# Token inputs laid out by feature on the host for a decoder layer on one core, in place of transposes at the kernel's start

## The chip, the cores and the metric

The kernel runs on one core of one Trainium2 chip. The metric is the device time of one execution in microseconds (us); lower is better. TensorE is PE in the rows of the profile (PEld is its weight load), VectorE is DVE, ScalarE is ACT, GpSimd is POOL and SyncE is SP. SP computes nothing here: it issues loads and stores, one after the other, and an issue that must wait holds up the issues behind it.

## The reference

One decoder layer on 256 tokens of 2048 features. Sixteen learned meta tokens are put in front, so 272 tokens go through the layer, and the sixteen are dropped at the end. All is float32.

```
s = concat(meta_tokens, x)                                   # 272 x 2048
h = rms_norm(s, norm_ffn1)
s = s + 0.5 * (silu(h @ w_gate_part) * (h @ w_up_part)) @ ffn1_w_down      # F = 5632
h = rms_norm(s, norm_mix)
q, k, v, b_gate, c_gate, u = split(h @ w_in)
y_att  = diff_attention(q, k, v, lam, subln)    # lam from four vectors of 64
y_conv = b_gate * conv3(c_gate * u, conv_w)
merged = sum over both branches of sigmoid(h @ w_gate) * (y @ w_branch)
s = s + merged @ w_out
h = rms_norm(s, norm_ffn2)
s = s + 0.5 * swiglu_ffn(h, ffn2_w_gu, ffn2_w_down)
out = rms_norm(s, norm_final)[16:]
```

The first product, `h @ ffn1_w_gu`, is where the change works; `ffn1_w_gu` is 2048 x 11264.

## The kernel before

**Layout.** The activations stand with features on the 128 partitions and tokens along the row: `sF[g]` holds four blocks of 128 features (chunks) by 272 tokens, and `s(c, t0)` is chunk c of 16. Products run with weights as the stationary operand, 128x128, and 272 tokens as the moving one.

**Two parts per operand.** Float32 values are split into a high and a low part, each in the format fp32r, and a product is made of three passes: high x high, low x high, high x low (lines 367 to 369). For weights, ACT makes the high part `wh` by a cast (lines 345 and 351) and DVE the low part `wl` by a subtraction (line 356). For activations `gain_split` multiplies by the norm's gain and splits: ACT makes the high part (line 231), DVE the low one (line 232). The factor of the norm that belongs to a token, `rstd`, is applied later, on the product.

**The first product.** `linear` walks 16 chunks of features and, for each, 4 blocks of 128 outputs: 16 x 4 x 3 = 192 passes, accumulated in four PSUM banks `pg`. In this first call a function `before1` prepares the activations while the product runs: chunk 0 alone, chunk 1 alone, then chunks in twos, each pair with one weight load `st` of 512 KB, one cast of 128x1024 and one subtraction of 128x1024. In the text below a pair is named by its chunks ("weights 2-3"). The squares for the norm are summed on the way: ACT squares a chunk (line 250), DVE adds it (line 252). After the last pass a product with ones (`ssq`, line 257) sums over partitions, and the next product, `pu`, starts at once.

**How the tokens come in.** x lies in memory by token. `load_x` brings 128 tokens by some chunks of features into `xin`; `prep` turns each 128x128 block by a transpose on PE (line 733) into the bank `pt`, and DVE copies it to `sF` (line 739). There are 16 chunks x 2 halves of the tokens = 32 such transposes and 16 copies. The meta tokens are turned two blocks at a time (line 724, bank `pm`) and copied in eight small pieces (line 727); the gain of the first norm is loaded as 16 rows and turned too (line 141). The other vectors (two norms, the convolution, `subln`) come by four small loads later, into `vrows`, and are turned in one transpose in `make_vec` (line 154) about 686 us into the run.

**What orders the start.** A scheduler orders instructions per engine from the program's order and the releases of buffers. SP's queue carries x and the weights alternately; ACT's queue carries the meta tokens and the gain. Seven products of ones (`keep_warm`, line 86) run on PE from the start, and two more behind the first transposes. There are four buffers `st`, three each of `wh` and `wl`, and eight PSUM banks.

**Names of the change.** `load_x`, `X_LOADS` (which chunks are loaded when), `prep`, `prep_meta`, `before1`, `load_vectors`, `make_vec`, `make_lam`.

Of the kernel before, what the change touches and what calls it, by code (L numbers as in the profile page):

```python
# [9 lines left out]
F32 = mybir.dt.float32  # L10
# [5 lines left out]
P = 128  # L16
D = 2048
SEQ = 256
NMETA = 16
# [3 lines left out]
GC = 4  # L23
# [14 lines left out]
N_AUX = 3  # L38
EVICT_AT = 1
WARM = 7  # L40
WARM_PREP = 2
HOLD = 6
LATER_AT = (4, 6)

# [16 lines left out]
def decoder_layer(ctx: ExitStack, tc: tile.TileContext, t, out):  # L61
# [9 lines left out]
    def bank(name):  # L71
        return psum.tile([P, 512], F32, tag="acc", name=name)
# [11 lines left out]
    def keep_warm(n):  # L84
        for _ in range(n):
            nc.tensor.matmul(warm[:, :P], ones, ones, start=True, stop=True)
# [1 line left out]
    keep_warm(WARM)  # L88


    grow = const.tile([DC, P], F32, name="grow")
    x = t["x"][0]
# [20 lines left out]
    vrows = const.tile([NV, P], F32, name="vrows")  # L113
    G_MIX, G_FFN2, G_CONV, G_SUB = 0, DC, 2 * DC, NV - 1

    lamv = tmp.tile([P, 4, HD], F32, tag="sc", name="lamv")
# [27 lines left out]
    vec = const.tile([P, NV], F32, name="vec")  # L144

    def col(i):
        return vec[:, i : i + 1]

    lam = const.tile([P, 40], F32, name="lam")[:, 0:1]
    subg = const.tile([P, 1], F32, name="subg")  # L150

    def make_vec():
        vp = bank("vp")
        nc.tensor.transpose(vp[:, :NV], vrows, ident[:NV, :NV])
# [14 lines left out]
    sF = [apool.tile([P, GC, T], F32, tag="act", name=f"s{g}") for g in range(DC // GC)]  # L169

    def s(c, t0, t1=T):
        return sF[c // GC][:, c % GC, t0:t1]

    class Act:

# [51 lines left out]
    def gain_split(h, c, gain):  # L227

        w = h.width
        hi, lo = h.part(c, 0, 0, w), h.part(c, 1, 0, w)  # L230
        a = nc.scalar.mul(hi, s(c, T - w), gain)  # L231
        b = nc.vector.scalar_tensor_tensor(  # L232
            out=lo, in0=s(c, T - w), scalar=gain, in1=hi.bitcast(F32), op0=ALU.mult, op1=ALU.subtract
        )
        return a.ins, b.ins
# [478 lines left out]
    h1 = Act("h1", DC, T, range(NH), PIECE)  # L714
    norm1 = Norm(0, "1")

    pm, split_of, turned = [], [], []

    def prep_meta(g):

        if not pm:
            pm.append(bank("pm"))
            for j in range(2):
                nc.tensor.transpose(pm[0][:, j * P : (j + 1) * P], xm[:, j * P : (j + 1) * P], ident)
        for j in range(2):
            cols = pm[0][:, j * P : (j + 1) * P].rearrange("p (t g) -> p g t", t=NMETA)
            nc.vector.tensor_copy(sF[g][:, j:GC:2, :NMETA], cols[:, 2 * g : 2 * g + 2, :])

    def prep(c):
        pt = bank("pt")  # L730
        q, cs = c // NH, slice(c % NH * P, (c % NH + 1) * P)
        for i in range(2):
            turned.append(nc.tensor.transpose(pt[:, i * P : (i + 1) * P], xin[q][i][:, cs], ident).ins)
        if c % GC == 0:
            prep_meta(c // GC)
        with ExitStack() as order:
            if c in (2, 3):
                order.enter_context(tc.issue_after(split_of[1]))
            v = nc.vector.tensor_copy(s(c, NMETA), pt[:, :SEQ])
        a, b = gain_split(h1, c, gain1[:, c : c + 1])  # L740
        split_of.append(b)
        return a, v.ins

    X_LOADS = {2: (2, 2), 4: (4, 4), 8: (8, 4), 10: (12, 4)}

    def before1(blk):


        c = blk[0]
        if c in X_LOADS:  # L750
            load_x(*X_LOADS[c])
        r = []
        for k in blk:
            a, v = prep(k)
            r = [a, v]
            if k == 0:
                r.append(split_of[0])
                with tc.issue_after(turned[-1]):
                    keep_warm(WARM_PREP)
        for k in blk:  # L760
            if k >= 2:
                norm1.add(k - 2)
        if c == DC - 2:
            for k in blk:
                norm1.add(k)
            pending.append(norm1.end)
        return r
# [538 lines left out]


_INS = [
    "x", "meta_tokens", "norm_ffn1", "ffn1_w_gu", "ffn1_w_down", "norm_mix", "w_in", "conv_w", "lambda_q1",
    "lambda_k1", "lambda_q2", "lambda_k2", "subln", "w_branch", "w_gate", "w_out", "norm_ffn2", "ffn2_w_gu",  # L1310
    "ffn2_w_down", "norm_final",
]


# [16 lines left out]
```

## Time and profile before

| what | value |
|---|---|
| runs of the kernel | 2149.14 us median of 3 (2148.92 to 2149.18) |
| profiled execution, span from first to last instruction | 2147.3 us |
| granted TensorE clock, mean | 0.999 |
| PE busy | 2137.4 us, 13202 instructions |
| DVE busy | 1611.9 us |
| ACT busy | 1105.5 us |
| bytes by DMA | 439.70 MB, mean 205 GB/s |

For the profiled execution itself only the span is on the page; the median of the runs is 1.84 us above it, which is what lies outside the first and last instruction. A busy share of an engine is a mean over the whole run; the change works in the first 37 us, and once at 686 us, so views restricted to a window are what to read. Starts are in us from the span's start. Consecutive instructions on an engine overlap at their ends, so the cost of one in a row of many is the distance from its start to the next start, which is a little less than its duration.

### The profile page before, as it was taken

To read this page: it belongs to the slowest core of one execution; us is meant where nothing else is said; L and a number is where in the kernel's file an instruction comes from. 1 tells how busy PE (TensorE), PEld (TensorE's weight loads), DVE (VectorE), ACT (ScalarE), POOL (GpSimd) and SP (SyncE) were. 2 spreads that over 40 slices of the span, in tenths; PEclk is the share of its full clock that TensorE was granted. 3 is DMA by queue.
4 is the path that set the end of the run, shared out by engine and by line. 5 is a ranking of instruction groups with operands and counts; after the bars stand their busy time and mean duration, and the time that the engine had idled before them with its cause. 6 is when DMAs were issued, how large, how long until landed. Compare 5 with 4: busy or idle time off the path is not lost.

```text
span 2147.3 us, 33079 instructions
## 1 busy us (share of the span) xinstructions
PE 2137.4 (100%) x13202; PEld 1929.1 (90%) x13202; DVE 1611.9 (75%) x2139; ACT 1105.5 (51%) x1391; POOL 79.4 (4%) x89
## 2 busy tenths in 40 slices
PE   9999999999999999999999999999999999999998
PEld 9999999999999998899988888888888888888887
DVE  8555554445555668867887889889999899988998
ACT  6344443344333455545545555557665566555665
POOL 0000000000000000000000000001100111012100
PEclk9999999999999999999999999999999999999999
DMA  7555555555555555544455555668886999779963
GB/s 258 177 177 178 177 181 177 178 180 179 180 180 176 178 178 187 190 157 142 154 189 186 198 201 187 216 206 256 267 259 198 286 285 277 234 219 311 287 207 138
DMA packets 200544, 439.70 MB, mean 205 GB/s; under 512 B 10493, under 2 KB 11206, under 8 KB 200390
## 3 DMA queue, kind: packets, MB, share of 16 engines
q1 hardware_dynamic: 184022, 398.13, 54.9%
q0 software_dynamic: 15904, 38.80, 8.2%
q8 instruction: 103, 1.69, 0.3%
q10 hardware_dynamic: 464, 0.66, 0.1%
q14 instruction: 51, 0.42, 0.1%
HBM read 431.26 MB, written 2.10 MB: 202 GB/s over the span
## 4 chain that ended last, share of the span: by engine, by line
PE 98%; DVE 1%; DMA 0%; ACT 0%; issue 0%; SPq 0%; ACTq 0%
PE pg L569 6%; PE pg L571 6%; PE pg L570 6%; PE pd L369 4%; PE pd L367 4%; PE pu L367 4%; PE pu L368 4%; PE pu L369 4%; PE pd L368 4%; PE pg L367 4%; PE pg L368 4%; PE pg L369 4%; PE pd L571 4%; PE pd L570 4%; PE pd L569 4%; PE g L571 2%
## 5 line engine op out<-in xcount | busy, mean ns | idle before, releaser
L356 DVE TENSOR_TENSOR wl<-st,wh 128x1024 fp32r<-128x1024 f32 (+1 forms) x329 | 401.1, 1221 | 378.4 <-ACT wh L351 378.3
L351 ACT CAST wh<-st 128x1024 fp32r<-128x1024 f32 (+1 forms) x328 | 343.0, 1047 | 487.4 <-PE pu L368 151.0
L476 DVE TENSOR_TENSOR wl<-st,wh 128x1024 fp32r<-128x1024 f32 (+1 forms) x424 | 470.9, 1118 | 55.4 <-ACT wh L475 52.3
L475 ACT CAST wh<-st 128x1024 fp32r<-128x1024 f32 (+1 forms) x424 | 400.3, 970 | 208.8 <-PE pdx L570 60.5
L475 ACT CAST wh<-t 128x1024 fp32r<-128x1024 f32 x160 | 166.6, 1052 | 242.5 <-DVE t L609 162.3
L476 DVE TENSOR_TENSOR wl<-t,wh 128x1024 fp32r<-128x1024 f32 x160 | 193.8, 1222 | 56.3 <-ACT wh L475 51.7
L369 PE MATMUL pd<-mh,wl 128*128 128x272 f32 x704 | 203.1, 288 | 0.0
L367 PE MATMUL pd<-mh,wh 128*128 128x272 f32 x704 | 202.3, 287 | 0.0
L367 PE MATMUL pu<-h,wh 128*128 128x272 f32 x704 | 201.9, 287 | 0.0
L367 PE MATMUL pg<-h,wh 128*128 128x272 f32 x704 | 201.6, 287 | 0.2 <-ACT h L231 0.2
L369 PE MATMUL pu<-h,wl 128*128 128x272 f32 x704 | 201.7, 287 | 0.0
L368 PE MATMUL pu<-h,wh 128*128 128x272 f32 x704 | 201.7, 286 | 0.0
L368 PE MATMUL pg<-h,wh 128*128 128x272 f32 x704 | 201.2, 287 | 0.1
L368 PE MATMUL pd<-ml,wh 128*128 128x272 f32 x704 | 200.7, 285 | 0.0
L369 PE MATMUL pg<-h,wl 128*128 128x272 f32 x704 | 199.6, 287 | 0.1
L570 PE MATMUL pg<-wh,h 128*128 128x512 f32 x399 | 156.0, 391 | 0.0
L569 PE MATMUL pg<-wh,h 128*128 128x512 f32 x399 | 155.8, 390 | 0.0
L571 PE MATMUL pg<-wl,h 128*128 128x512 f32 x399 | 155.7, 391 | 0.0
L368 PEld LDWEIGHTS pd<-ml,wh 128*128 128x128 f32 x704 | 133.5, 190 | 0.0
L367 PEld LDWEIGHTS pg<-h,wh 128*128 128x128 f32 x704 | 132.6, 188 | 0.7 <-ACT h L231 0.4
L368 PEld LDWEIGHTS pg<-h,wh 128*128 128x128 f32 x704 | 132.6, 188 | 0.3 <-DVE h L232 0.3
L368 PEld LDWEIGHTS pu<-h,wh 128*128 128x128 f32 x704 | 132.6, 188 | 0.0
(391 smaller groups left out, 4839.6 us busy)
## 6 DMA issues: line engine op xcount, KB each, us to landing
st<-in_ffn_w_gu_dram SPq DMA_DIRECT2D x183, 512.0 KB, 6.0
st<-in_ffn_w_down_dram SPq DMA_DIRECT2D x88, 1024.0 KB, 5.1
st<-in_ffn_w_gu_dram SPq DMA_DIRECT2D x84, 1024.0 KB, 4.9
st<-in_w_in_dram SPq DMA_DIRECT2D x48, 1024.0 KB, 5.1
st<-in_w_gate_dram SPq DMA_DIRECT2D x64, 512.0 KB, 4.1
t<-in_ffn_w_gu_dram POOLq DMA_DIRECT2D x64, 512.0 KB, 7.0
st<-in_w_branch_dram SPq DMA_DIRECT2D x32, 512.0 KB, 4.5
st<-in_w_out_dram SPq DMA_DIRECT2D x16, 1024.0 KB, 5.2
```

The lines of the kernel that those rows point to most:

```text
L351: nc.scalar.copy(out=wh[:, :m, :], in_=sw)
L356: nc.vector.tensor_sub(wl[:, :m, :], sw, wh[:, :m, :].bitcast(F32))
L367: nc.tensor.matmul(a, wh[:, i, f], act.part(c, 0, t0, t1), start=first, stop=False)
L368: nc.tensor.matmul(a, wh[:, i, f], act.part(c, 1, t0, t1), start=False, stop=False)
L369: nc.tensor.matmul(a, wl[:, i, f], act.part(c, 0, t0, t1), start=False, stop=last)
L475: part_last[:] = [nc.scalar.copy(out=wh, in_=src).ins]
L476: part_last.append(nc.vector.tensor_sub(wl, src, wh.bitcast(F32)).ins)
L569: nc.tensor.matmul(ps[k], hi, wh, start=first, stop=False)
L570: nc.tensor.matmul(ps[k], lo, wh, start=False, stop=False)
L571: nc.tensor.matmul(ps[k], hi, wl, start=False, stop=left[k] == 0)
```

## The change

The host now hands over x and the meta tokens as one array of 128 x 16 x 272 (partition, chunk, token), the gain of the first norm as 128 x 16, and the other vectors as one array of 128 x 57. `load_x` writes straight into `sF`; the transposes, the banks and the copies are gone, and so are the two extra products of ones. The first chunk of x comes on ACT's queue, after the gain; all others on SP's queue. (Line numbers of the new kernel are smaller: line 99 is `load_x`, 205 and 206 are the two halves of `gain_split`, 226 the addition of squares, 311 the weight load, 325 the cast, 330 the subtraction, 341 to 343 the three passes.)

```diff
-WARM_PREP = 2
...
-    xm = apool.tile([P, 2 * P], F32, tag="act", name="xm")
-    xin = [[apool.tile([P, W2], F32, tag="act", name=f"xin{q}{i}") for i in range(2)] for q in range(2)]
...
-    def load_x(c, n):
-
-        q, cs = c // NH, slice(c % NH * P, (c % NH + n) * P)
-        for i in range(2):
-            x_load[:] = [
-                nc.sync.dma_start(out=xin[q][i][:, cs], in_=x[i * P : (i + 1) * P, c * P : (c + n) * P]).ins
-            ]
-
-    load_x(0, 2)
-    meta_load = nc.scalar.dma_start(out=xm, in_=t["meta_tokens"].rearrange("t (g f) -> (t g) f", f=2 * P))
-    with tc.issue_after(meta_load.ins):
-        nc.scalar.dma_start(out=grow, in_=t["norm_ffn1"][0].rearrange("(c p) -> c p", p=P))
+    def load_x(c, n, eng=None):
+        dst = sF[c // GC][:, c % GC : c % GC + n, :]
+        ins = (eng or nc.sync).dma_start(out=dst, in_=x[:, c : c + n, :]).ins
+        if eng is None:
+            x_load[:] = [ins]
+
+    gain1 = const.tile([P, DC], F32, name="gain1")
+    nc.scalar.dma_start(out=gain1, in_=t["gain1"])
+    load_x(0, 1, nc.scalar)
...
     def load_vectors():
-        for g0, src in ((G_MIX, t["norm_mix"][0]), (G_FFN2, t["norm_ffn2"][0])):
-            nc.sync.dma_start(out=vrows[g0 : g0 + DC, :], in_=src.rearrange("(c p) -> c p", p=P))
-        nc.sync.dma_start(
-            out=vrows[G_CONV:G_SUB, :], in_=t["conv_w"][0].rearrange("k (c p) -> (k c) p", p=P)
-        )
-        nc.sync.dma_start(out=vrows[G_SUB:NV, :], in_=t["subln"])
+        nc.sync.dma_start(out=vec, in_=t["vectors"])
...
-    gp = bank("gp")
-    nc.tensor.transpose(gp[:, :DC], grow, ident[:DC, :DC])
-    gain1 = const.tile([P, DC], F32, name="gain1")
-    nc.vector.tensor_copy(gain1, gp[:, :DC])
...
-    def make_vec():
-        vp = bank("vp")
-        nc.tensor.transpose(vp[:, :NV], vrows, ident[:NV, :NV])
-        nc.vector.tensor_copy(vec, vp[:, :NV])
...
     def prep(c):
-        pt = bank("pt")
-        q, cs = c // NH, slice(c % NH * P, (c % NH + 1) * P)
-        for i in range(2):
-            turned.append(nc.tensor.transpose(pt[:, i * P : (i + 1) * P], xin[q][i][:, cs], ident).ins)
-        if c % GC == 0:
-            prep_meta(c // GC)
-        with ExitStack() as order:
-            if c in (2, 3):
-                order.enter_context(tc.issue_after(split_of[1]))
-            v = nc.vector.tensor_copy(s(c, NMETA), pt[:, :SEQ])
-        a, b = gain_split(h1, c, gain1[:, c : c + 1])
-        split_of.append(b)
-        return a, v.ins
-
-    X_LOADS = {2: (2, 2), 4: (4, 4), 8: (8, 4), 10: (12, 4)}
+        return gain_split(h1, c, gain1[:, c : c + 1])
+
+    X_LOADS = {0: (1, 1), 1: (2, 2), 2: (4, 2), 4: (6, 2), 6: (8, 4), 8: (12, 4)}
...
         for k in blk:
-            a, v = prep(k)
-            r = [a, v]
-            if k == 0:
-                r.append(split_of[0])
-                with tc.issue_after(turned[-1]):
-                    keep_warm(WARM_PREP)
+            r = list(prep(k))
...
-            side.extend((make_vec, make_lam))
+            side.append(make_lam)
...
+    tokens = np.concatenate([a["meta_tokens"], a["x"][0]], axis=0)
+    d["x"] = tokens.T.reshape(DC, P, T).transpose(1, 0, 2)
```

Three places of the program show how rows move. The first is SP's queue at the start of the program. `xin` holds tokens by token, `s` is the tile `sF`, `st` a weight load; 128x256 is a row of 1 KB per partition. Before:

```order
L104 DMA xin_90<-in_x_dram 128x256
L104 DMA xin_91<-in_x_dram 128x256
L337 DMA st<-in_ffn_w_gu_dram 128x512 x2
L104 DMA xin_90<-in_x_dram 128x256
L104 DMA xin_91<-in_x_dram 128x256
L337 DMA st<-in_ffn_w_gu_dram 128x2x512
```

And now:

```order
L311 DMA st<-in_ffn_w_gu_dram 128x512
L99 DMA s_88<-in_x_dram 128x272
L99 DMA s_88<-in_x_dram 128x544
L311 DMA st<-in_ffn_w_gu_dram 128x512
L99 DMA s_89<-in_x_dram 128x544
L311 DMA st<-in_ffn_w_gu_dram 128x2x512
```

The first weights come ahead of x, and three pieces of x (chunks 1, 2-3 and 4-5) stand ahead of weights 2-3, where four pieces (chunks 0-1 and 2-3, two each) stood before.

The second place is PE's start. `warm` is the bank of the products of ones. Before:

```order
L86 MATMUL warm<-ones 128x128 x7
L141 MATMUL gp<-ident,grow 128x16
L733 MATMUL pt<-ident,xin_90 128x128
L733 MATMUL pt<-ident,xin_91 128x128
L724 MATMUL pm<-ident,xm 128x128 x2
L86 MATMUL warm<-ones 128x128 x2
L733 MATMUL pt<-ident,xin_90 128x128
L733 MATMUL pt<-ident,xin_91 128x128
L367 MATMUL pg_145<-h_116,wh 128x272
```

And now:

```order
L85 MATMUL warm<-ones 128x128 x7
L341 MATMUL pg_133<-h_104,wh 128x272
L341 MATMUL pg_134<-h_104,wh 128x272
L341 MATMUL pg_135<-h_104,wh 128x272
L341 MATMUL pg_136<-h_104,wh 128x272
L342 MATMUL pg_133<-h_104,wh 128x272
```

Between the seven products of ones and the first real pass PE has nothing left to do.

The third place is DVE's queue behind its two memsets, where `norm` is the sum of squares. Before:

```order
L143 COPY gain_107<-gp 128x16
L739 COPY s_112<-pt 128x256
L727 COPY s_112<-pm 128x2x16 x2
L727 COPY s_113<-pm 128x2x16 x2
L232 SCALAR_TENSOR_TENSOR h_116<-s_112,gain_107,h_116 128x272
L356 TENSOR_TENSOR wl<-st,wh 128x512
L739 COPY s_112<-pt 128x256
```

And now:

```order
L206 SCALAR_TENSOR_TENSOR h_104<-s_88,gain_92,h_104 128x272
L330 TENSOR_TENSOR wl<-st,wh 128x512
L206 SCALAR_TENSOR_TENSOR h_104<-s_88,gain_92,h_104 128x272
L330 TENSOR_TENSOR wl<-st,wh 128x512
L206 SCALAR_TENSOR_TENSOR h_105<-s_88,gain_92,h_105 128x272 x2
L226 TENSOR_TENSOR norm<-norm 128x272
L330 TENSOR_TENSOR wl<-st,wh 128x1024
```

What is left on DVE is the low parts and the additions, in the same order among themselves up to small shifts.

More of the change, by code (lines that the diff above doesn't have):

```diff
@@ L88, in decoder_layer, with s @@
     keep_warm(WARM)
-    grow = const.tile([DC, P], F32, name="grow")
-    x = t["x"][0]
-    xm = apool.tile([P, 2 * P], F32, tag="act", name="xm")
-    xin = [[apool.tile([P, W2], F32, tag="act", name=f"xin{q}{i}") for i in range(2)] for q in range(2)]
+    x = t["x"]
     x_load = []
-    def load_x(c, n):
-        q, cs = c // NH, slice(c % NH * P, (c % NH + n) * P)
-        for i in range(2):
-            x_load[:] = [
-                nc.sync.dma_start(out=xin[q][i][:, cs], in_=x[i * P : (i + 1) * P, c * P : (c + n) * P]).ins
-            ]
-    load_x(0, 2)
-    meta_load = nc.scalar.dma_start(out=xm, in_=t["meta_tokens"].rearrange("t (g f) -> (t g) f", f=2 * P))
-    with tc.issue_after(meta_load.ins):
-        nc.scalar.dma_start(out=grow, in_=t["norm_ffn1"][0].rearrange("(c p) -> c p", p=P))
+    sF = [apool.tile([P, GC, T], F32, tag="act", name=f"s{g}") for g in range(DC // GC)]
+    def s(c, t0, t1=T):
+        return sF[c // GC][:, c % GC, t0:t1]
+    def load_x(c, n, eng=None):
[6 more added lines that the diff above has]
+    load_x(0, 1, nc.scalar)
     NV = 2 * DC + 3 * NH + 1
-    vrows = const.tile([NV, P], F32, name="vrows")
     G_MIX, G_FFN2, G_CONV, G_SUB = 0, DC, 2 * DC, NV - 1
+    vec = const.tile([P, NV], F32, name="vec")
     lamv = tmp.tile([P, 4, HD], F32, tag="sc", name="lamv")
     def load_vectors():
-        for g0, src in ((G_MIX, t["norm_mix"][0]), (G_FFN2, t["norm_ffn2"][0])):
-            nc.sync.dma_start(out=vrows[g0 : g0 + DC, :], in_=src.rearrange("(c p) -> c p", p=P))
-        nc.sync.dma_start(
-            out=vrows[G_CONV:G_SUB, :], in_=t["conv_w"][0].rearrange("k (c p) -> (k c) p", p=P)
-        )
-        nc.sync.dma_start(out=vrows[G_SUB:NV, :], in_=t["subln"])
+        nc.sync.dma_start(out=vec, in_=t["vectors"])
         for i, n in enumerate(("lambda_q1", "lambda_k1", "lambda_q2", "lambda_k2")):
@@ L1308, with _by_partition, _laid_out @@
 _INS = [
-    "x", "meta_tokens", "norm_ffn1", "ffn1_w_gu", "ffn1_w_down", "norm_mix", "w_in", "conv_w", "lambda_q1",
-    "lambda_k1", "lambda_q2", "lambda_k2", "subln", "w_branch", "w_gate", "w_out", "norm_ffn2", "ffn2_w_gu",
-    "ffn2_w_down", "norm_final",
-]
+    "ffn1_w_gu", "ffn1_w_down", "w_in", "lambda_q1", "lambda_k1", "lambda_q2", "lambda_k2", "w_branch", "w_gate",
+    "w_out", "ffn2_w_gu", "ffn2_w_down", "norm_final",
+]
+def _by_partition(np, a):
+    rows = a.reshape(-1, a.shape[-1] // P, P)
+    return np.ascontiguousarray(rows.reshape(-1, P).T)
+def _laid_out(np, inputs):
+    a = {k: np.asarray(v) for k, v in inputs.items()}
+    d = {name: a[name] for name in _INS}
+    tokens = np.concatenate([a["meta_tokens"], a["x"][0]], axis=0)
+    d["x"] = tokens.T.reshape(DC, P, T).transpose(1, 0, 2)
+    d["gain1"] = _by_partition(np, a["norm_ffn1"])
+    d["vectors"] = np.concatenate(
+        [_by_partition(np, v) for v in (a["norm_mix"], a["norm_ffn2"], a["conv_w"][0], a["subln"])], axis=1
+    )
+    return d
 def kernel(**inputs):
@@ L1321 @@
     arrays, args = {}, {}
-    for name in _INS:
-        a = _np.ascontiguousarray(inputs[name])
+    for name, a in _laid_out(_np, inputs).items():
+        a = _np.ascontiguousarray(a)
         arrays[f"in_{name}_dram"] = a
```

13 lines of the change are left out of this document (removed).

## The prediction

> **What bounds the kernel.** I read the page first, for which engine the run hangs on.
>
> ```profile
> span 2147.3 us, 33079 instructions
> ...
> PE 98%; DVE 1%; DMA 0%; ACT 0%; issue 0%; SPq 0%; ACTq 0%
> ```
>
> The chain that ended last runs over PE for 98% of the span. So whatever shortens PE's queue, or lets it start earlier, comes off the end, unless something else becomes late. The 2% that are not PE lie mostly at the start; the same chain, restricted to the first 37 us, shows what:
>
> ```profile
> 1.19 3.06 DMA xin<-in_x_dram
> ...
> 4.66 6.65 DMA xin<-in_x_dram
> ...
> 11.35 0.34 PE pt L733
> ...
> 12.47 0.72 DVE wl L356
> ...
> 30.42 0.34 DVE s L739
> ...
> 36.13 0.46 PE ssq_ps L257 x2
> 36.59 0.12 PE pu L367
> ```
>
> First a load of x sets the pace (its second piece lands at 11.3), then for 19 us DVE, with copies from `pt` (L739) among the low parts, and from there PE. The next product starts at 36.59. Two windows over PE's passes, of `pu` and of `pg` from chunk 2 on, tell what the stage costs beyond its products:
>
> ```profile
> 36.59:60.30 23.71, 23.68 (x192) 23.46 (x191) 0.80 (x3) 1.00 0.61 205
> 12.09:36.13 24.04, 22.64 (x168) 21.18 (x168) 0.00 (x0) 0.00 (x0) 1.00 0.81 281
> ```
>
> With nothing in the way 192 passes take 23.71 us, 0.1235 each. Chunks 2 to 15 are 168 passes, 20.75 us at that rate, but stand from 12.09 to 36.13, 24.04 us: 3.3 us go to transposes and waits. After 36.59 PE is never short of work for long, so I take the start of `pu` as the finish line: the run ends as much earlier as `pu` starts earlier.
>
> **The change, part by part.** *Transposes on PE.* The timeline of PE:
>
> ```profile
> 1.06 3.35 PE L86 MATMUL warm<-ones 128*128 128x128 f32 x14 [1.06 <-DVE ones L80]
> 4.56 0.69 PE L733 MATMUL pt<-ident,xin 128*128 128x128 f32 x2
> 5.46 0.66 PE L86 MATMUL warm<-ones 128*128 128x128 f32 x4
> 5.96 0.38 PE L733 MATMUL pt<-ident,xin 128*128 128x128 f32 x2
> 6.51 0.39 PE L367 MATMUL pg<-h,wh 128*128 128x272 f32 x1 [0.16 <-ACT h L231]
> 8.87 0.60 PE L733 MATMUL pt<-ident,xin 128*128 128x128 f32 x4
> 10.88 0.27 PE L733 MATMUL pt<-ident,xin 128*128 128x128 f32 x1
> 11.35 0.98 PE L733 MATMUL pt<-ident,xin 128*128 128x128 f32 x7 [0.20 <-DMA xin<-in_x_dram]
> 12.09 0.37 PE L367 MATMUL pg<-h,wh 128*128 128x272 f32 x1
> ```
>
> A lone transpose shows 0.27, seven in a row 0.98, so one more costs (0.98 - 0.27) / 6 = 0.118 us. Up to 12.09 there are 2 + 2 + 4 + 1 + 7 = 16 of 32; the other 16 lie in the window from 12.09, 1.9 us. Of its 3.3 us that leaves 1.4 us of waits.
>
> *Copies on DVE.* The DVE timeline gives the price of each kind by the distance of starts:
>
> ```profile
> 12.39 1.22 DVE L356 TENSOR_TENSOR wl<-st,wh 128x1024 fp32r<-128x1024 f32 x1
> ...
> 23.55 0.90 DVE L232 SCALAR_TENSOR_TENSOR h<-s,gain,h 128x272 fp32r<-128x272 f32 x2
> 24.38 0.43 DVE L252 TENSOR_TENSOR norm<-norm 128x272 f32<-128x272 f32 x1
> 24.73 1.21 DVE L356 TENSOR_TENSOR wl<-st,wh 128x1024 fp32r<-128x1024 f32 x1
> 25.87 0.43 DVE L252 TENSOR_TENSOR norm<-norm 128x272 f32<-128x272 f32 x1
> 26.22 0.74 DVE L739 COPY s<-pt 128x256 f32<-128x256 f32 x2
> 26.89 0.42 DVE L252 TENSOR_TENSOR norm<-norm 128x272 f32<-128x272 f32 x1
> ...
> 34.10 1.22 DVE L356 TENSOR_TENSOR wl<-st,wh 128x1024 fp32r<-128x1024 f32 x1
> ```
>
> A low part of h is 0.415, an addition 0.35, a subtraction 1.14, a copy 0.335. From 12.39 to the end of the subtraction at 34.10 (35.3) DVE has 8 x 1.14 + 12 x 0.415 + 14 x 0.35 + 10 x 0.335 = 22.4 us of work in 22.9: it is full, and nearly as long as PE's stage. Without the copies 19.0 are left, under PE's 20.75, so behind chunk 2 the bound passes to PE. Not all 1.4 us of waits go: a pair's eight passes with `wh` last 1.0 us, while its subtraction, which the ninth pass needs, takes 1.14 behind the cast, so where cast and pass come due together 0.2 to 0.35 is lost; I count two such places and keep 0.6. Two numbers follow: the finish line lies 20.75 + 0.6 + 0.46 (`ssq`) = 21.8 us behind the first pass of chunk 2, against 36.59 - 12.09 = 24.5 before. Gain: 2.7 us, with 1.9 to 3.3 as bounds (only the transposes, or no wait at all).
>
> *Start of chunk 2.* Before, 12.09. Now it hangs on weights 2-3, which must land and be cast. The cast, from the ACT timeline, and the loads, from the view of DMA issues (x's first piece, weights 2-3) and SP's timeline:
>
> ```profile
> 10.93 1.03 ACT L351 CAST wh<-st 128x1024 fp32r<-128x1024 f32 x1
> ...
> xin<-in_x_dram SPq DMA_DIRECT2D x1, 128.0 KB, 3.0
> st<-in_ffn_w_gu_dram SPq DMA_DIRECT2D x1, 512.0 KB, 5.7
> ...
> 3.73 0.38 SPq L337 DMA_DIRECT2D st<-in_ffn_w_gu_dram  x1
> ```
>
> Weights 2-3 were issued at 3.73 and landed at 9.43. What SP's queue moved, counted from 0 to 5.5, 6.5, 7, 8 and 9 us (packets, MB):
>
> ```profile
> q1 hardware_dynamic: 564, 0.75, 49.3%
> q1 hardware_dynamic: 828, 1.04, 55.5%
> q1 hardware_dynamic: 928, 1.19, 59.4%
> q1 hardware_dynamic: 1109, 1.53, 64.1%
> q1 hardware_dynamic: 1245, 1.79, 67.8%
> ```
>
> Before, weights 2-3 ended 1536 KB of that queue (x 512, weights 1024), 1.57 MB, moved by 8.1; they landed 1.3 us later. Now they end 1704 KB (weights 256, x 136 and 272, weights 256, x 272, weights 512), 1.75 MB, moved by 8.8 at the same pace, so they land at 10.1. Counted in rows of a partition instead, it is 896 now against 1024 before: reached at 6.85 and 7.5, so that they would land about 8.7. The two views differ because the rows of x are now longer. From 5.5 to 6.5 us, with rows of 1 KB among them, 264 packets carried 0.29 MB, from 7 to 8 us 181 carried 0.34: the packets differ by half, the bytes by a sixth, so bytes are nearer to what limits, and I take 9.8. With 1.05 for the cast chunk 2 starts at 10.85: gain 1.25, bounds 2.3 (rows) and 0.6 (0.3 later by bytes, and the slower clock below).
>
> *The first pass.* At 6.51 before. Now the first weights are first in SP's queue and chunk 0 second in ACT's; by the 3.0 us above, and the 1.19 + 3.06 in the chain for a second piece, both land by about 4.3, cast and high part follow, and the first pass comes at 5.4. That 1.1 us is not added: chunks 0 and 1 end by 10 either way, and chunk 2 waits for its weights. SP's issue times don't bind, since weights 2-3 are its sixth issue.
>
> *Late vectors.* One transpose less at 686 us, and the wait of DVE for the last small load, in the rows of `vp` and of `lamv`:
>
> ```profile
> L154 PE MATMUL vp<-ident,vrows x1: 269/269/269, 685.6 to 685.6; 57*128 57x57 f32 x1
>   DMA lamv<-in_lambda_k_dram: 0.4, 1
> ```
>
> The transpose is worth 0.1 us by the price above. Four small loads become one, and the scaled `subln` now comes on DVE at 277 us, next to the product that waited 0.4 us there; three loads fewer ahead of it can only shorten that. PE covers it; uncovered it costs 0.4. The gain's load of 64 bytes per partition stands ahead of chunk 0 on ACT's queue, where 8 KB stood behind the meta tokens; 8 KB either way, taken at nothing, and at most the 1.1 us of the first pass.
>
> *Sum.* 2.7 + 1.25 + 0.1 = 4.05 us off the profiled span of 2147.3, and so off the median, 1.84 above it: 2149.14 - 4.05 = 2145.1. 0.2% of the time, 4.3 us, is about what a measurement of this kernel can tell from no change, so the likeliest case lies just inside it.
>
> **Rivals.** *Loads go by rows.* Weights 2-3 land at 8.7, chunk 2 starts at 9.75, and the gain is 2.3 + 2.7 + 0.1 = 5.1: 2144.0. For it: the new rows of x are 1 to 4 KB where half of the early rows were 1 KB. Against: the counts of packets and bytes above.
>
> *Late or slow first chunks.* The passes of ones run 3.35 / 14 = 0.24 us each at 1.06, and four of them take 0.66 at 5.46, (0.66 - 0.27) / 3 = 0.13: PE got twice as fast at about 5.3, though the granted clock reads 1.00 throughout. Now PE has nothing between 4.4 and 5.4, and gaps again around chunks 0 and 1. If it is at half rate there, 24 passes of 0.247 from 5.4 end at 11.5 with a small wait, so chunk 2 starts at 11.5: gain 0.6 + 2.7 + 0.1 = 3.4, 2145.7. If it stays so for 14 more passes, 1.7 us go and the gain is 1.7: 2147.4. The Trainium skill, "TensorE: Matmul & The Clock Gate", section "What's actually happening", has the array at half rate until about 3.4 us of sustained work fill a window that runs freely, and again after an idle window. This trace agrees as to the factor and roughly as to the time, 4.2 us from the first pass; by that rule the idle microsecond may or may not spoil the window, and the second variant would be one more window.
>
> *Slower.* The same mechanism, but without recovery: PE keeps half rate until the product is dense. Each pass then costs 0.12 more; from 11.5 on 28 passes eat the gain (to 18.4 us), and 62 make it slower by 0.2% (to 27 us). At 30 us it would be 75 passes, 9.3 us: 2155.0. Against it: the passes from 11.5 on are dense, and before the change 4.2 us of them were enough.
>
> *The transposes were hidden anyway.* If x's loads bound the start as before and chunk 2 starts at 12.09, only 2.8 are gained: 2146.3. The chain above speaks for loads at the start, but weights 2-3 landed at 9.43, and it was x that came at 11.3.
>
> **How the numbers follow.** As forecast (gain 3.5 to 4.6): 0.45. By rows (4.6 to 5.7): 0.25. Slow first chunks or late loads (1.5 to 3.5): 0.26. Slower: 0.04. The range takes the first two whole and the third down to a gain of 2.3: 2143.4 to 2146.8. Faster by over 0.2% is the second case and some 0.4 of the first: 0.42. Slower by over 0.2%: 0.03. The rest, 0.55, within it.
>
> **What would show it.** `pu` starts at 32.6 instead of 36.59; chunk 2's first pass at 10.85, released by ACT's cast, and that by the load of weights 2-3; DVE idle at times between 12 and 32 instead of full; passes of chunks 0 and 1 about 0.12 apart (0.25 for the slow clock). Wrong it would be if weights 2-3 land before 9 or after 11, if DVE remains the chain's engine behind chunk 2, or if anything behind `pu` shifts by more than some tenths.

## The result and the profile after

The changed kernel takes 2144.64 us (median of 13 runs, 2144.09 to 2144.95) where the kernel before took 2149.09 in the same session (13 runs, 2148.78 to 2150.06): a ratio of 0.9979, 95% interval 0.9972 to 0.9986, or 4.45 us less. The forecast was 2145.1, with 4.05 us less. The profiled execution of the changed kernel is the quickest of its 13 (2144.09 us), so the two profiled spans lie 5.0 us apart instead of 4.45; sums over the two traces are made against 5.0.

The page of the changed kernel: its span, the busy times, and the engines on the chain that ended last.

```profile
span 2142.3 us, 32969 instructions
...
PE 2132.4 (100%) x13162; PEld 1925.7 (90%) x13162; DVE 1604.8 (75%) x2113; ACT 1105.5 (52%) x1391; POOL 79.3 (4%) x89
...
PE 99%; DMA 0%; DVE 0%; ACT 0%; issue 0%; ACTq 0%
```

The chain restricted to the first 36 us has nothing of DVE left in it. It is one load of x, the high part of chunk 0 on ACT, and from 5.02 on PE without a gap (start, length, what):

```profile
1.18 3.17 DMA s<-in_x_dram
4.44 0.53 ACT h L205
5.02 1.27 PE pg L341 x4
...
9.69 0.18 PE pg L342
9.88 0.13 PE pg L343
...
31.17 0.46 PE ssq_ps L231 x2
```

The timeline of PE gives the first pass, its releaser, the first pass of chunk 2, and the two landmarks at the end of the stage, displayed by start:

```profile
5.02 1.27 PE L341 MATMUL pg<-h,wh 128*128 128x272 f32 x4 [0.60 <-ACT h L205]
...
10.22 0.28 PE L341 MATMUL pg<-h,wh 128*128 128x272 f32 x1
...
31.00 0.62 PE L231 MATMUL ssq_ps<-norm,ones 128*128 128x272 f32 x2
31.26 0.49 PE L341 MATMUL pu<-h,wh 128*128 128x272 f32 x1
```

Before, the same timeline has:

```profile
35.97 0.62 PE L257 MATMUL ssq_ps<-norm,ones 128*128 128x272 f32 x2
36.23 0.49 PE L367 MATMUL pu<-h,wh 128*128 128x272 f32 x1
```

So `pu` starts 4.97 us earlier, and the spans differ by 5.0: what lies behind `pu` did not change by more than the 0.1 that the spans are given to. Two windows over the passes of `pg` (length, then busy time and count on PE, PEld, DVE, ACT, the granted clock, DMA share, GB/s) show where the stage is short and where it is not:

```profile
5.02:9.70 4.68, 4.68 (x20) 4.68 (x21) 0.00 (x0) 0.00 (x0) 1.00 1.05 392
...
10.40:31.13 20.73, 20.73 (x168) 20.54 (x167) 0.00 (x0) 0.00 (x0) 1.00 0.92 329
```

The 168 passes of chunks 2 to 15 take 20.73 us, the 0.1235 apiece of a PE that waits for nothing. (Their first starts at 10.22 in the timeline, while the pass ahead of it still ends; the window begins where that one has ended. Below, chunk 2 is put at 10.22, since the 12.09 of the kernel before is a start in the timeline too.) The first 20 passes take 0.234 each, though the granted clock reads 1.00: PE was at half rate until 9.7. And DVE, with no copies, is no longer full. The same stretch before (first row) and after (second; columns PE, PEld, DVE, ACT, POOL):

```profile
12.00:31.00 19.00, 18.74 (x153) 18.37 (x151) 19.00 (x40) 13.87 (x29) 0.00 (x0) 1.00 0.80 290
```

```profile
12.00:31.00 19.00, 19.00 (x155) 18.99 (x155) 16.71 (x30) 14.88 (x29) 0.00 (x0) 1.00 0.91 322
```

Weights 2-3, whose landing the forecast put at 9.8, were issued on SP's queue at 3.07 and took 5.2 us, so they landed at 8.27, and their cast followed at once. The rows are from SP's timeline, the view of DMA issues and ACT's timeline:

```profile
3.07 0.43 SPq L311 DMA_DIRECT2D st<-in_ffn_w_gu_dram  x1
```

```profile
st<-in_ffn_w_gu_dram SPq DMA_DIRECT2D x1, 512.0 KB, 5.2
```

```profile
8.26 1.04 ACT L325 CAST wh<-st 128x1024 fp32r<-128x1024 f32 x1
```

The cast ended at 9.3, and PE, busy with chunks 0 and 1 until then, took chunk 2 at 10.22.

### The profile page after: what moved, and what is told of

The parts are those of the page before. It is cut to its first block, busy times and chain, and to the rows that moved or that the text cites. A ratio compares the mean times of both kernels' runs of the same rounds, so it can differ in the third digit from the quotient of the medians.

```text
span 2142.3 us, 32969 instructions
## 1 busy us (share of the span) xinstructions
PE 2132.4 (100%) x13162; PEld 1925.7 (90%) x13162; DVE 1604.8 (75%) x2113; ACT 1105.5 (52%) x1391; POOL 79.3 (4%) x89
## 4 chain that ended last, share of the span: by engine, by line
PE 99%; DMA 0%; DVE 0%; ACT 0%; issue 0%; ACTq 0%
PE pg L543 6%; PE pg L545 6%; PE pg L544 6%; PE pd L343 4%; PE pg L341 4%; PE pg L343 4%; PE pg L342 4%; PE pd L341 4%; PE pu L341 4%; PE pu L343 4%; PE pu L342 4%; PE pd L342 4%; PE pd L545 4%; PE pd L544 4%; PE pd L543 4%; PE g L545 2%
```

## The experiments

The theory after this reading: the gain is a start about 1.5 us earlier and the transposes gone from PE; PE's half rate at the start took the place of waits that vanished. Its rivals: that the half rate costs time, that the loads' rows or order made the gain, that DVE's copies did. Each kernel had 9 to 11 timed runs beside the kernel before on the same chip, which stood at 2149.05 to 2149.16. The intervals of the ratios are some 0.001 to either side, 2 us; a smaller difference between two of these kernels is one of medians from different chips, and stands only as far as the ranges of their runs lie apart.

**Products of ones.** Three kernels change only the number of pairs of products of ones at the program's start (7 in the changed kernel); with 8 and 10 no other instruction changes its place in its queue.

```
-WARM = 7
+WARM = 8      (second kernel: 10; third: the call left out)
```

> The changed kernel with eight products of ones instead of seven, so that PE's idle stretch from 4.41 to 5.02 us is filled (a product of ones takes 0.48 us at the slow rate; the eighth ends at 4.9). In the changed kernel PE's passes stand 0.23 us apart until 9.6 us and 0.12 apart after. Theory A (the idle stretch of 0.6 us makes the count of busy time start anew): PE becomes fast at about 5.3 us, as before the change, chunk 2 starts when weights 2-3 are cast, at 9.4 instead of 10.4, and the next product starts at 30.6 instead of 31.6: 2143.6. Theory B (the time of the switch is not tied to that stretch): the switch comes anywhere, the next product starts at 31.6, and the time stays at 2144.6.

> Ten products of ones instead of seven: PE is busy without a break from 1.06 to about 5.6. Theory A: PE becomes fast at about 5.3 us, the first real pass comes some 0.5 later than in the changed kernel, at 5.6, but at the fast rate; chunk 2 at 9.4, next product at 30.6, 2143.6. Theory B: the two or three products too many delay the first pass to 5.9 at the slow rate, and chunk 2 and the next product by as much: 32.4, 2145.4.

> No products of ones at all. If only what runs without a break before the switch counts (theory A), the seven products before the stretch of 0.6 us give nothing in the changed kernel, PE becomes fast at 9.6 again, the next product starts at 31.6 and the time is 2144.6. If they count in part, the switch comes later: at half rate until 13 us the passes up to then lose another 1.7 us, so 33.3 and 2146.3.

Measured: 2144.37 us with eight pairs (ratio to before 0.9977, 0.9968 to 0.9986), 2144.50 with ten (0.9978, 0.9970 to 0.9987), 2145.30 with none (0.9982, 0.9973 to 0.9991). The last is 0.7 more than the changed kernel, with runs of 2144.92 to 2146.03 against 2144.09 to 2144.95; the first two are not told from it. With eight pairs the time and the start of `pu` (31.56) are those of theory B; with ten and with none neither expected time came. But with eight and ten pairs PE did get fast, as theory A had it. PE's timeline with eight pairs:

```profile
5.67 0.70 PE L342 MATMUL pg<-h,wh 128*128 128x272 f32 x4
...
9.65 0.39 PE L341 MATMUL pg<-h,wh 128*128 128x272 f32 x1 [0.46 <-ACT wh L325]
...
31.31 0.62 PE L231 MATMUL ssq_ps<-norm,ones 128*128 128x272 f32 x2
```

A group of four passes shows 0.70 where the changed kernel showed 1.11. Chunk 2 then starts at 9.65 instead of 10.22, and `ssq_ps` all the same at 31.31 instead of 31.00. What became of the 0.57 us? The chain of that kernel:

```profile
2.12 4.39 DMA st<-in_ffn_w_gu_dram
6.53 0.62 ACT wh L325
7.15 0.84 ACT h L205 x2
...
12.50 0.42 DVE wl L330
...
19.07 1.23 DVE wl L330
20.34 0.77 PE pg L343 x4
```

From the start of chunk 2 to `ssq_ps` it is 21.66 us instead of 20.78: 0.9 us of waits. The chain runs from the landing of weights 1 over casts on ACT and low parts on DVE up to 20.34, and only then into PE. So the rival that the half rate costs time falls, as far as 20 passes go: a fast PE arrives early and waits for what a slow PE found ready. Only without any products of ones, where the slow passes last until 11.3 (some 28 of them), does the half rate reach the end.

**Transposes and copies put back.** The first kernel turns each chunk over on PE into a bank that nobody reads; the second adds a DVE copy of each result into a tile that nobody reads. The third loads x into a tile of its own, turns it over as the first does, and has DVE copy each chunk into `s` before its high part is made.

```
 def prep(c):
+    pt = bank("pt")
+    for i in range(2):
+        nc.tensor.transpose(pt[:, i*P:(i+1)*P], s(c, NMETA + i*P, NMETA + (i+1)*P), ident)
+    nc.vector.tensor_copy(scratch[:, :SEQ], pt[:, :SEQ])            # second kernel
+    nc.vector.tensor_copy(s(c, 0), xR[c // GC][:, c % GC, :])       # third kernel
```

> The changed kernel with the 32 transposes of x put back on PE, each reading the piece of x that it waits for, their result not used; no copies on DVE. At 0.118 us each, 28 of them behind the first pass are 3.3 us, and four ahead of it some 0.5. Theory: PE is what bounds the stage, without a wait between chunk 2 and the next product, so nearly all shows: next product at 35 instead of 31.6 (34.5 if transposes help PE to become fast earlier), 2147.6 to 2148.1. Rival: the transposes fall into PE's waits for loads and casts and cost under 2 us: 2146.6 or less, and then it was the copies on DVE that the change saved.

> The 32 transposes of x stand on TensorE as in the run with them alone (2147.6 us), and after each pair VectorE copies the 128x256 result out of PSUM into a tile that nobody reads: 16 copies. Theory: VectorE was full in the kernel before because of them; 16 x 0.335 = 5.4 us of copies use up its idle time and the rest is waited for, so the start of pu moves from 34.4 to 35.5-36.3 and the time to 2148.6-2149.4, which together with the transposes gives the whole gain back. Rival: TensorE with the transposes is the bound and covers the copies: pu at 34.4 to 34.8 and 2147.5-2148.0; then 1.2 us or more of the gain came from elsewhere, the order of the loads.

> The changed kernel's loads go to a tile of their own; TensorE turns each chunk of it over (32 transposes, read by nobody), and VectorE copies each chunk from there into s, 16 copies of 128x272, ahead of the chunk's high part on ACT: as in the kernel before, x cannot be used until VectorE has copied it. With the transposes alone it was 2147.6, with copies that nobody waits for 2147.8. If the copies' place in the chain gave the other 1.3 us of the gain, this is 2148.7-2149.3, with waits for h around chunks 1 to 4. If not, it is within 0.5 us of 2147.8, and the order and the layout of the loads are left.

Measured: 2147.58 us with the transposes (0.9991, 0.9982 to 1.0001), 2147.84 with copies beside them (0.9994, 0.9985 to 1.0003), 2147.77 with copies in the chain (0.9994, 0.9986 to 1.0003). The transposes cost 2.94 us, as expected. The copies cost 0.26 and 0.19, less than these runs tell from nothing: of the two outcomes set down for each, the one came in which the copies are covered. The waits of PE for other engines up to the end of the stage (total, times, longest) in the second kernel:

```profile
PE pt L694 <- DVE pcopy L695: 1.3, 1, 1.3
PE pg L343 <- DVE wl L330: 0.2, 1, 0.2
```

The copies do hold PE up for 1.3 us, at 11.4 ahead of chunk 2, but behind that the passes run densely. In the kernel with transposes alone PE waited 1.0 us for low parts instead, so most of the wait only changed its place; in the two traces `ssq_ps` lies 0.56 apart. And DVE with the copies shows no idle time from 12 to 31 us, as in the kernel before (columns as above):

```profile
12.00:31.00 19.00, 19.00 (x157) 19.00 (x157) 19.00 (x41) 14.14 (x27) 0.00 (x0) 1.00 0.87 291
```

From 12 us on PE waited for it no more: a DVE that is full is not yet one that PE waits for. None of the three contains the small copies of the meta tokens or a first pass that must wait for a transpose.

**The order and the rows of the loads.** Five kernels. Two move weights 1 and 2-3 ahead of a piece of x in SP's queue, one with seven and one with eight pairs of ones. One stores x with gaps, so that the same loads move rows of 544 bytes.

```
-X_LOADS = {0: (1, 1), 1: (2, 2), 2: (4, 2), 4: (6, 2), 6: (8, 4), 8: (12, 4)}
+X_LOADS = {0: (1, 1), 2: (2, 2), 4: (4, 2), 6: (6, 2), 8: (8, 4), 12: (12, 4)}
...
-ins = (eng or nc.sync).dma_start(out=dst, in_=x[:, c : c + n, :]).ins          # the third kernel
+ins = (eng or nc.sync).dma_start(
+    out=dst.rearrange("p c (h t) -> p (c h) t", h=2), in_=x[:, 2 * c : 2 * (c + n), : T // 2]
+).ins                                                                          # rows of 136 in 152
```

> SP's queue carries weights 1 ahead of x's chunks 2-3, and weights 2-3 ahead of chunks 4-5, with every later piece of x moved back likewise. Seven pairs of products of ones as in the changed kernel, whose PE ran its first 20 passes at half rate and waited for nothing behind 5.0 us. Theory: weights land earlier (1 at 5.4 instead of 6.2, 2-3 at 7.5 instead of 8.3), but PE does not wait for them; the time stays at 2144.6 +- 0.4 as long as PE starts slow. Rival: the order of loads, casts and low parts sets the start of pu whatever PE's rate: pu about 0.8 us earlier, 2143.8.

> The same order of loads with eight pairs of products of ones, with which PE ran its first passes at 0.13 to 0.15 us each. Theory: with a fast PE the chain is weights 1 landed (6.5 with eight pairs before), its cast, then ACT and VectorE in turn; weights 1 land 0.8 us earlier, so pu starts 0.6-1.0 us earlier than with eight pairs alone (30.6-31.0 where that showed 31.56), and the time is 2143.5-2143.9. Rival: ACT's and VectorE's work up to the last low part is the bound by its length, not by its start, and the later x delays it in turn: pu at 31.3 or later and 2144.2 or more.

> The same bytes of x in the same loads, but stored in the device's memory with a gap after each half chunk, so that each row that a load moves is 544 bytes instead of 1088 to 4352. Up to and with weights 2-3 SP's queue then has 1792 rows instead of 896, and 1704 KB in either case. If rows set the pace (about 1109 packets by 8 us in both kernels), weights 2-3 land at 10.5-11.5 instead of 8.27, chunk 2 waits for them, and pu starts 1.0-2.5 us later: 2145.6-2147.1. If bytes do, they land within 0.5 us of 8.3 and the time stays at 2144.6 +- 0.4.

Measured: 2143.81 us (0.9976, 0.9966 to 0.9985), 2143.70 with eight pairs (0.9975, 0.9965 to 0.9984), and 2145.38 with short rows (0.9982, 0.9974 to 0.9991). The earlier weights are worth 0.8 us on the medians with seven pairs and 0.7 with eight; the runs of the two kernels (2143.36 to 2144.18 and 2143.10 to 2143.99) hardly overlap those without the move (2144.09 to 2144.95 and 2144.18 to 2144.75). For the first the rival's time came, but the trace shows only a third of it: PE is at half rate at first there too, waits for nothing behind its first pass, and `ssq_ps` starts 0.27 us earlier, because the rate doubles 0.5 us earlier. For the second the expected time came. There a new wait shows on ACT's timeline: the high parts of chunks 2 and 3 stand waiting for x, which now comes behind the weights, and the cast of weights 2-3 is queued behind them:

```profile
7.05 0.94 ACT L205 ACTIVATE h<-s,gain 128x272 fp32r<-128x272 f32 x2 [0.63 <-DMA s<-in_x_dram]
...
8.53 1.03 ACT L325 CAST wh<-st 128x1024 fp32r<-128x1024 f32 x1
```

The short rows decide between rows and bytes. What SP's queue had moved by 9 us (packets, MB), first in the changed kernel, then with short rows, and for these the issue of weights 2-3 on SP and the time to their landing:

```profile
q1 hardware_dynamic: 1314, 2.39, 76.2%
```

```profile
q1 hardware_dynamic: 2514, 2.24, 77.1%
```

```profile
3.18 0.51 SPq L313 DMA_DIRECT2D st<-in_ffn_w_gu_dram  x1
```

```profile
st<-in_ffn_w_gu_dram SPq DMA_DIRECT2D x1, 512.0 KB, 5.5
```

Nearly twice the packets, 6% fewer bytes. Even that is hardly told from scatter: the eight kernels whose loads are those of the changed one moved 2.26 to 2.39 MB by then. Weights 2-3 landed at 8.68, 0.4 later, not 2 to 3. Rows do not set the pace here. The time, though, lies 0.4 us above the 2144.6 +- 0.4 that stood for this outcome: the first pass came 0.2 later, and the half rate lasted until 10.4 instead of 9.7.

The other two kernels give each layout the other's order of loads.

```
 (kernel before)
-load_x(0, 2)
+load_x(0, 1, nc.scalar)      # ahead of the meta tokens on ACT's queue
+x_load.clear()
-X_LOADS = {2: (2, 2), 4: (4, 4), 8: (8, 4), 10: (12, 4)}
+X_LOADS = {0: (1, 1), 1: (2, 2), 2: (4, 2), 4: (6, 2), 6: (8, 4), 8: (12, 4)}
 (changed kernel: the same lines the other way round)
```

> The kernel before, with tokens on partitions, its transposes and its copies, but with the loads in the order of the changed kernel: chunk 0 of x first on ACT's queue, weights 0 first on SP's, then x by one or two chunks between the weights. 1.3 us of the gain were left unexplained by transposes (2.9) and by copies that nobody waits for (0.3). If the order of the loads is what gave them, this kernel gains 1.0-1.5 us: 2147.6-2148.1. If they came from the copies standing between the load of x and its high part, or from what the loads of tokens move in rows of 512 to 1024 bytes, it stays within 0.4 us of 2149.1, or gets slower because the gain of the norm now comes behind on ACT's queue.

> The changed kernel with the order of loads of the kernel before: chunks 0-1 of x first on SP's queue, weights 0 and 1 behind them, the rest of x in four, four and four chunks. If the order gave the 1.3 us, this kernel loses them: 2145.6-2146.1, with the first pass at 5.8 or later and PE waiting for loads. If the order is worth little, the first pass comes 0.3-0.5 us later than 5.02, PE runs on from there at half rate and then without waits, and the time is 2144.6-2145.1.

Measured: 2150.99 us for the kernel before in the new order (1.0009, 1.0000 to 1.0017), slower by 1.9 on the medians with an interval that reaches 1, and 2145.34 for the changed kernel in the old order (0.9983, 0.9974 to 0.9992), 0.7 worse than in its own. Neither matches the loss or gain of 1.3 that was asked for, and both traces say what else the order did. In the first, the gain of the norm is the fourth load on ACT's queue, and PE's transposes of x stand in PE's queue behind the transpose of that gain. PE's timeline, and the wait of SP:

```profile
5.78 0.26 PE L142 MATMUL gp<-ident,grow 16*128 16x16 f32 x1 [1.37 <-DMA grow<-in_norm_ffn_dram]
5.97 0.69 PE L734 MATMUL pt<-ident,xin 128*128 128x128 f32 x2
...
8.02 0.57 PE L368 MATMUL pg<-h,wh 128*128 128x272 f32 x1
...
37.52 0.62 PE L258 MATMUL ssq_ps<-norm,ones 128*128 128x272 f32 x2
```

```profile
SPq L104 <- DMA xin<-in_x_dram: 2.0, 1, 2.0
```

The first pass comes at 8.02 instead of 6.51, 1.51 later, and `ssq_ps` 1.55 later. SP stood 2.0 us waiting for a load of ACT's queue. The program shows why: over both queues the loads take eight semaphores in turn, and from the ninth load on an issue waits until the load that had its semaphore has landed. In SP's part of that program (two halves of x per piece, so the loads are many and small; four of the eight are ACT's) the wait comes at SP's fifth load:

```
DMA xin 128x256 [waits DMAHW0]
DMA st 128x512 [waits DMAHW1]
```

By 9 us its queue had moved 1.25 MB, against 1.79 before and 2.39 in the changed kernel:

```profile
q1 hardware_dynamic: 1185, 1.25, 53.0%
```

The first eight loads carry 776 KB there (64, 64, 128 and 8 on ACT's queue; 256, 64, 64 and 128 on SP's), 1160 in the kernel before, 1848 in the changed one, 2632 in the changed one with the old order. Over both queues 1.52, 1.93, 2.54 and 2.49 MB had moved by 9 us. So up to the changed kernel the bytes rise with what eight loads hold, and beyond it they do not. That the eight loads are the cause is not shown: a kernel that changes only the number of loads was not run, and in the kernel before the packets filled 0.94 of the time of the 16 DMA engines from 5 to 9 us, against 1.04 in the changed one, a smaller difference than that of the bytes. The two rows are from before and after (the last two columns are this DMA share and GB/s):

```profile
5.00:9.00 4.00, 3.61 (x24) 2.94 (x23) 3.22 (x13) 2.47 (x6) 0.00 (x0) 1.00 0.94 288
```

```profile
5.00:9.00 4.00, 3.98 (x17) 3.99 (x18) 3.43 (x7) 3.12 (x7) 0.00 (x0) 1.00 1.04 386
```

In the changed kernel with the old order the first instruction on ACT waits for x, and ACT's table load of 1.28 us comes only behind that wait, where the kernel before and the changed kernel make it while nothing has landed yet. The chain up to the first pass:

```profile
0.74 2.78 DMA s<-in_x_dram
...
3.60 1.28 ACT L205
...
4.89 0.52 ACT h L205
5.41 0.51 ACT wh L319
5.92 0.43 ACT h L205
...
6.40 1.28 PE pg L341 x4
```

x has landed at 3.5, 0.8 earlier than in the changed kernel, but the table load, a high part, the cast of weights 0 and another high part follow one another on ACT, and the first pass is at 6.40, 1.38 late. What the order of the loads alone would do is not separated by this kernel. Of the 1.38, 1.10 are left at `ssq_ps` and 0.7 on the clock.

**ACT's and DVE's work.** The last kernel makes the square of chunk 0 only, with eight pairs of ones; the other 15 squares and their additions are left out, so its norm is not that of the layer.

```
-        if k >= 2:
-            norm1.add(k - 2)
+        if k == 2:
+            norm1.add(0)
...
-        for k in blk:
-            norm1.add(k)
```

> Eight pairs of products of ones (2144.37 us, PE at full rate from its first pass, chunk 2 at 9.65 behind ACT, 1.1 us of waits for low parts after it), and of the squares for the first norm only that of chunk 0 is made: 15 squares less on ACT (0.32 each) and 15 additions less on VectorE (0.35 each). If the work of ACT and VectorE is what keeps a PE at full rate from starting pu earlier, chunk 2 starts at 8.9-9.1, nothing is waited for behind it, and pu starts at 29.8-30.2 instead of 31.56: 2142.6-2143.0. If the loads or the casts and subtractions alone hold it, pu stays at 31.0 or later and the time at 2143.8 or more.

Measured: 2144.64 us (0.9979, 0.9970 to 0.9988), no gain over 2144.37. It does not settle its question. With the sum of squares done early, the rest of the norm moved into the stage as well: a table load of 1.28 us and an activation on ACT, and on DVE a reciprocal ahead of a subtraction that PE then waited for (1.2 us in all):

```profile
18.29 1.85 DVE L255 RECIPROCAL rstd<-rsa 128x272 f32<-128x272 f32 x1
20.05 3.43 DVE L330 TENSOR_TENSOR wl<-st,wh 128x1024 fp32r<-128x1024 f32 x3
```

## Why the prediction was right, and where its steps were not

One ledger holds all kernels but that last one. From the first pass to `ssq_ps` PE must do 192 passes (23.7 us at 0.1235) and the transposes that are left (28 of 32 at 0.118, 3.3 us). What remains is lost, to half rate or to waits:

| kernel | first pass | transposes | `ssq_ps` | lost | us |
|---|---|---|---|---|---|
| before | 6.51 | 3.3 | 35.97 | 2.5 | 2149.1 |
| after | 5.02 | 0 | 31.00 | 2.3 | 2144.64 |
| eight ones | 5.07 | 0 | 31.31 | 2.5 | 2144.37 |
| ten ones | 5.13 | 0 | 31.28 | 2.5 | 2144.50 |
| no ones | 5.00 | 0 | 31.88 | 3.2 | 2145.30 |
| transposes back | 5.04 | 3.3 | 34.18 | 2.1 | 2147.58 |
| with copies | 5.02 | 3.3 | 34.74 | 2.7 | 2147.84 |
| copies in chain | 5.22 | 3.3 | 34.90 | 2.7 | 2147.77 |
| weights ahead | 5.05 | 0 | 30.73 | 2.0 | 2143.81 |
| and eight ones | 5.05 | 0 | 30.87 | 2.1 | 2143.70 |
| rows of 544 bytes | 5.23 | 0 | 31.49 | 2.6 | 2145.38 |
| before, new order | 8.02 | 3.3 | 37.52 | 2.5 | 2150.99 |
| after, old order | 6.40 | 0 | 32.10 | 2.0 | 2145.34 |

The change is 1.49 (first pass) + 3.3 (transposes) + 0.2 (less lost) = 5.0 us of the profiled spans. What is lost is a remainder, from one trace of each kernel; it lies between 2.0 and 2.7 in all of them but the one without ones. The forecast cut the same 5.0 at another place, the start of chunk 2: 1.87 ahead of it (12.09 to 10.22) and 3.10 behind.

*Finish line.* Right: the start of `pu` and the end shifted alike, by 4.97 and 5.0.

*Behind chunk 2.* 2.7 forecast, 3.1 measured: from the start of chunk 2 to that of `pu` it was 36.23 - 12.09 = 24.14 and is 31.26 - 10.22 = 21.04. The transposes were sized rightly (1.9 of it; 2.94 for all of them on the clock). The waits before were 1.2 rather than 1.4, since the pass at 12.09 starts 0.24 before the seven transposes ahead of it end (11.35 + 0.98). The 0.6 us of waits kept for late subtractions did not come; by the rows because PE reached chunk 2 late, with the subtractions ahead. In the run with eight pairs, where PE came early, 0.9 us of waits came. That DVE would stop being full was right, 16.71 of 19.00 us. That the copies on a full DVE were what made PE wait is not borne out: put back, they cost 0.2 to 0.3, with DVE full again.

*Start of chunk 2.* 1.25 forecast, 1.87 measured, and not by the step given. Weights 2-3 landed at 8.27, not 9.8, which is also ahead of the 9 that was named as a sign of being wrong; and it was not their cast, ended at 9.3, that released the first pass of chunk 2, but PE's own queue. The assumption that failed is that bytes flow at the same pace as before: from 2 to 5 us they flowed at 320 GB/s instead of 257, from 5 to 9 us at 386 instead of 288. The rival by rows had a nearer time (8.7), for a reason that the run with short rows does not bear out. Of the 1.16 us by which these weights landed earlier, 0.66 is their issue, at 3.07 instead of 3.73: they are SP's sixth load now and were its seventh, and as the ninth of both queues that one also waited 0.2 us until the first piece of x (0.74 + 3.0) had landed. The forecast counted bytes alone. The other 0.5 is a quicker way (5.2 us instead of 5.7), whose cause stays open.

*The first pass, "not added".* This is the step that failed. It came at 5.02, not 5.4, and its 1.49 us are in the gain: they are the larger part of the 1.87. The argument was that chunk 2 must wait for its weights; but the weights were early and PE was slow, so chunks 0 and 1 ran straight on from the first pass. By the rows, the 1.49 have two causes, and either alone would have left the other standing; that is argued, not tested. In the kernel before ACT's cast of weights 0 waited for them until 5.35, and the copy of chunk 0 and the small ones of the meta tokens, of which its high part needs the first, ended about when the cast did (DVE's timeline, then ACT's):

```profile
5.28 0.42 DVE L739 COPY s<-pt 128x256 f32<-128x256 f32 x1 [0.44 <-PE pt L733]
5.71 0.48 DVE L727 COPY s<-pm 128x32 f32<-128x32 f32 x4
```

```profile
5.35 0.62 ACT L345 CAST wh<-st 128x512 fp32r<-128x512 f32 x1 [2.40 <-DMA st<-in_ffn_w_gu_dram]
5.93 0.52 ACT L231 ACTIVATE h<-s,gain 128x272 fp32r<-128x272 f32 x1
```

Now weights 0 are first in the queue and cast at 3.58, and x, landed at 4.35, is used at 4.44. How much each of the two gives alone was not separated: the two runs with exchanged orders each moved something else as well. What the 1.49 are worth on the clock is not settled either: the transposes put back leave 1.5 us of the gain of 4.45, but a first pass 1.38 later cost only 0.7 in the changed kernel with the old order.

*The rival of slow first chunks.* Its mechanism came, its price did not. 20 passes ran at half rate, 2.2 us of them, but no more was lost than before (2.3 against 2.5), since a PE at full rate waits about as long for casts and low parts (2.5 lost with eight and with ten pairs). Its second variant, in which the half rate lasts longer, is the run with no ones: 0.9 us more lost, 0.7 on the clock. The Trainium skill, "TensorE: Matmul & The Clock Gate", section "What's actually happening", has the switch come after a busy window of about 3.4 us, and has the moment vary by about 0.5 us because the windows run freely. The traces agree as to the factor (0.234 to 0.1235) but not as to the moment: without ones it came 6.3 us after the first pass, in the changed kernel 4.7 us after it, though 3.35 us of ones stood ahead.

*The other rivals.* That the transposes were hidden anyway falls with the run that put them back (2.94 us). The half rate did not persist: it ended at 9.7, far from the 18.4 at which it would have eaten the gain.

*Late vectors.* 0.1 forecast; `pu` and the span differ by 0.03 in their shift, less than the display tells.

*Sum.* 4.05 against 4.45 on the medians, and against 5.0 on the profiled executions, of which that of the changed kernel is 0.55 below its median. Both large terms were too small, 2.7 against 3.1 and 1.25 against 1.87, and the second came by another way than the one given: the earlier first pass, put at nothing, makes most of it. The mechanism is borne out for the transposes alone, some two thirds of the gain; that the time lies within half a microsecond of the forecast is in part luck.

## What to carry to other kernels

Make the ledger first: when the first product starts, how long the products are without gaps, and what is lost between; a term that moves the first product counts until something is shown that takes it back. Waits and half rate at a kernel's start can cover each other, as here (2.3 us lost with the one, 2.5 with the other), so that removing one of them shows little. When loads at the start are many and small, look which of them must wait to be issued, and for what, before arguing with bytes or rows.

## What the runs showed of the hardware that was not expected

- Rows of 544 bytes for x instead of 1088 to 4352 hardly changed the bytes moved by 9 us (2.24 MB on SP's queue, against 2.26 to 2.39 in eight kernels with the same loads and long rows). The kernel before with the new order, whose first loads of x are 64 and 128 KB instead of 136 and 272, moved 1.25 MB there, with SP waiting 2.0 us to issue.
- ACT's first table load took 1.28 us in every one of the kernels looked at here. In the kernel before and in the changed one it ran at 1.67 and 1.66, ahead of ACT's first wait; in the changed kernel with the old order it ran at 3.60, behind the wait of ACT's first instruction for x, and so stood on the way to the first pass.
- PE's rate doubled at a different moment in nearly every trace (before or in the first passes with ten pairs, in two of three kernels with eight, and in two of three with transposes put back; at 6.1 in the third with eight; at 9.2, 9.7, 10.4 and 11.3 us in others), while the granted clock read 1.00 throughout. There is one trace of each kernel, so how much of this is the kernel and how much the execution stays open.
